# Sigmoid products, a Relu kept in PSUM and a key mask added by TensorE, in a hybrid decoder layer

## The chip, the cores and the metric

The kernel runs on one NeuronCore of a Trainium2 chip. The metric is the device time of one execution in microseconds (us). Engines are named as in the profile: PE is TensorE (matrix products), PEld its weight loads, DVE is VectorE, ACT is ScalarE, POOL is GpSimd, and SP is the engine whose queue issues most DMAs.

## The reference

One layer for 512 tokens of width 1024: a half-step SwiGLU, a mixer with two attention groups of 8 heads of 64, a second half-step SwiGLU, each with norms and modulation around it. The change touches the mixer alone. What it must compute there:

```
# group A: an indexer chooses 128 keys for each query, softmax over those
sc    = relu(einsum('bthd,bsd->bths', q_idx, k_idx))
score = where(causal, einsum('bths,bth->bts', sc, w_idx), -inf)
idx   = top_k(score, 128)
logits = q.k[idx] * D**-0.5 + rel_bias[t5_bucket(t - idx)]   # -inf where t - idx < 0
out   = softmax(logits) @ v[idx]

# group B: stick-breaking attention
z     = q.k * D**-0.5            # keys s < t only
A[t,s] = sigmoid(z_ts) * prod over s < j < t of sigmoid(-z_tj)
out   = A @ v
```

## The kernel before

Everything is float32; a product keeps its precision by three TensorE passes over operands split into a rounded high part (type fp32r) and a remainder (L271 to L273). A row block is 128 queries, `i` = 0 to 3, and it sees `L = 128 * (i + 1)` keys, so a head has four blocks of 128, 256, 384 and 512 columns, 1280 in all.

The mixer runs in this order. First the indexer (`indexer`): for 8 index heads and blocks `i` = 1 to 3 it forms 24 score tiles. Each is two products into a PSUM bank (L787, L788), a Relu by ACT from the bank into an SBUF tile `rl` (L734), and a product with the head's weight added to the running score by DVE (L735). Then `topk` takes the 128 largest of each row in sixteen rounds of MAX8 and MATCH_REPLACE8 on DVE (L766, L769) and leaves `notsel`, a bf16 tile with 1 where a key is not chosen (L772).

Then come eight units of two heads: units 0 to 3 are group B, 4 to 7 group A. While a unit's attention runs, the projections q, k, v of the next unit are slipped in between by `fill` (groups of L271 to L273), so PE has work whenever the attention waits. The weights of these projections are split by ACT or POOL and POOL (L132, L133, L138 `wl<-raw,wh`). The topk rounds have no data to wait for in group B and are slipped in on DVE there.

A block of a group B head (`attn_b`): two products and a bf16 product that masks the diagonal block (L895), then `Abs`, `Exp`, `Ln` on ACT (L897 to L899), `max(z, 0)` on ACT or DVE (L901, L903), a sum from the right by a scan on DVE (L904, two SBUF inputs), a subtraction (L905) and a last `Exp` on ACT (L906).

A block of a group A head (`attn_a`): DVE first builds `b` = bias window + mask in SBUF for all four blocks (L919, two SBUF inputs). Then two products (L787, L788), an addition with a running maximum (L926, which the profile calls CUSTOM_DVE_ANT_0), a negation of the maximum (L928) and `Exp` with the sum of the row on ACT (L929).

After that, in both groups, PE turns the weights around (L882), ACT and DVE split them (L132, L138 `pt`), and PE multiplies by v (L857). At the change of groups `bias_windows` makes the bias windows `U` by way of DRAM and `o_norm` normalizes group B's output (POOL's power, L143, then L574, L202, L577).

The order on each engine is set when the program is built, by a scheduler that hoists what it thinks is ready; on the chip each engine runs its list in order. Tiles come from pools. Those that matter: three PSUM banks `at` hold score tiles, attention tiles and the product with v; three SBUF tiles `p` of 128x1280 are shared by `x` and `y` in group B and by `p` and `b` in group A; `rl` has three buffers.

Of the kernel before, what the change touches and what calls it, by code (L numbers as in the profile page):

```python
# [13 lines left out]
F32 = mybir.dt.float32  # L14
F32R = mybir.dt.float32r
BF16 = mybir.dt.bfloat16
AF = mybir.ActivationFunctionType
ALU = mybir.AluOpType
# [5 lines left out]
NT = S // 128  # L24
# [6 lines left out]
NEG = -1e30  # L31
# [6 lines left out]
P_OFF = [0, 128, 384, 768]  # L38
# [26 lines left out]
class Block:  # L65
# [605 lines left out]
    def indexer(self):  # L671

        nc, pool, pj, at, tp, small, n = self.nc, self.pool, self.pj, self.at, self.tp, self.small, self.n
        w_in, ident = self.d["w_in"], self.ident
        cm = pool.tile([128, 512], BF16, tag="cm", name="cm")
# [6 lines left out]
                            nc.gpsimd if j < 2 else None), 128) for j in range(3)]  # L682
        banks = [pj.tile([128, 512], F32, tag="mm", name="mm") for _ in range(3)]
        banks.append(at.tile([128, 512], F32, tag="at", name="at"))
        load = nc.scalar.preload_act_table_set("natural_log_exp_and_others")
        self.tc.keep_in_program_order(load)
        wix = pool.tile([128, NT, NH], F32, tag="wix", name="wix")
        ki, qi = [], []
# [38 lines left out]
        def scores(hd):  # L727
            def one(i):
                L = 128 * (i + 1)
                s = sco[i - 1][:, 0:L]  # L730
                ps = at.tile([128, 512], F32, tag="at", name="at")[:, 0:L]
                self.qk(ps, i, hd % 2, qi[hd // 2], (kih, kih), (kil, kil), True)
                rl = pool.tile([128, 512], F32, tag="w2", name="rl", bufs=3)[:, 0:L]
                nc.scalar.activation(rl, ps, AF.Relu)  # L734
                nc.vector.scalar_tensor_tensor(s, rl, wix[:, i, hd:hd + 1], cm[:, 384 - 128 * i:512] if hd == 0 else s,  # L735
                                               op0=ALU.mult, op1=ALU.add)
            return [lambda i=i: one(i) for i in range(1, NT)]

        w3 = self.w_cols(w_in, C_QI + 384, 128)
        ps = pj.tile([128, 512], F32, tag="mm", name="mm")  # L740
# [9 lines left out]
        notsel, tops = [self.tri_gt], []  # L750
        for i in range(1, NT):
            L = 128 * (i + 1)
            ns = pool.tile([128, 512], BF16, tag=f"ns{i}", name="ns")
            tops.append(self.topk(sco[i - 1][:, 0:L], ns[:, 0:L]))
            notsel.append(ns)
# [130 lines left out]
    def attn_b(self, hd, qk):  # L886

        nc, pool, at = self.nc, self.pool, self.at
        x = pool.tile([128, 1280], F32, tag="p", name="x", bufs=3)
        y = pool.tile([128, 1280], F32, tag="p", name="y", bufs=3)  # L890
        for i in range(NT):
            L = 128 * (i + 1)
            ps = at.tile([128, 512], F32, tag="at", name="at")
            self.qk(ps[:, 0:max(256, L)], i, hd, *qk, False)
            nc.tensor.matmul(ps[:, 128 * i:L], self.negi, self.tri_ge, start=False, stop=True)  # L895
            z, xs, ys = ps[:, 0:L], x[:, P_OFF[i]:P_OFF[i] + L], y[:, P_OFF[i]:P_OFF[i] + L]
            nc.scalar.activation(xs, z, AF.Abs)  # L897
            nc.scalar.activation(xs, xs, AF.Exp, scale=-1.0)
            nc.scalar.activation(xs, xs, AF.Ln, bias=1.0)  # L899
            if i < 2:  # L900
                nc.scalar.activation(ys, z, AF.Relu)  # L901
            else:
                nc.vector.tensor_scalar(ys, z, 0.0, None, op0=ALU.max)  # L903
            nc.vector.tensor_tensor_scan(ys[:, ::-1], ys[:, ::-1], xs[:, ::-1], 0.0, op0=ALU.add, op1=ALU.add)  # L904
            nc.vector.tensor_sub(xs, z, ys)  # L905
            nc.scalar.activation(xs, xs, AF.Exp)  # L906
            self.fill()
        return x

    def attn_a(self, hd, qk, bias, notsel, den):  # L910

        nc, pool, at, small = self.nc, self.pool, self.at, self.small
        p = pool.tile([128, 1280], F32, tag="p", name="p", bufs=3)
        mx = small.tile([128, 4], F32, tag="mx", name="mx", bufs=2)
        nm = small.tile([128, 4], F32, tag="nm", name="nm", bufs=2)
        b = pool.tile([128, 1280], F32, tag="p", name="b", bufs=3)
        for i in range(NT):
            L = 128 * (i + 1)
            nc.vector.scalar_tensor_tensor(b[:, P_OFF[i]:P_OFF[i] + L], notsel[i][:, 0:L], NEG,  # L919
                                           bias[:, 0:L][:, ::-1], op0=ALU.mult, op1=ALU.add)  # L920
        for i in range(NT):
            L = 128 * (i + 1)
            ps = at.tile([128, 512], F32, tag="at", name="at")
            self.qk(ps[:, 0:max(256, L)], i, hd, *qk, True)
            pp = p[:, P_OFF[i]:P_OFF[i] + L]
            nc.vector.tensor_tensor_reduce(out=pp, in0=ps[:, 0:L], in1=b[:, P_OFF[i]:P_OFF[i] + L], scale=1.0,  # L926
                                           scalar=-3e38, op0=ALU.add, op1=ALU.max, accum_out=mx[:, i:i + 1])
            nc.vector.tensor_scalar(nm[:, i:i + 1], mx[:, i:i + 1], -1.0, None, op0=ALU.mult)  # L928
            nc.scalar.activation(pp, pp, AF.Exp, bias=nm[:, i:i + 1], accum_out=den[:, i, hd:hd + 1])  # L929
            self.fill((0, 1, 1, 2)[i])  # L930
        return p

# [33 lines left out]
```

## Time and profile before

| | us |
|---|---|
| median of 3 runs | 1123.7 (1123.42 to 1124.68) |
| the profiled execution, its own time | 1124.37 |
| its span | 1122.6 |
| PE busy | 1064.0 (95%) |
| DVE busy | 627.5 (56%) |
| ACT busy | 433.4 (39%) |
| POOL busy | 168.8 (15%) |

The first SwiGLU and the mixer's norm end near 430 us, the indexer runs to about 483, group B to about 604, group A to about 712, and the output projection and the second SwiGLU fill the rest. A matrix product of 512 columns is shown as about 395 ns long, but the next one starts 230 ns later, so the durations overlap: the start times tell what PE delivers, and a busy PE may still be held up.

### The profile page before, as it was taken

What the parts mean: (1) busy time and instruction counts of PE and PEld (TensorE: products, weight loads), DVE (VectorE), ACT (ScalarE), POOL (GpSimd) and SP (SyncE); (2) the same over time, 40 slices, a digit from 0 to 9 for tenths busy, and PEclk for the clock granted to TensorE, in tenths of its full rate; (3) what the DMA queues carried; (4) which work ended last, traced back from release to release, by engine and by line L of the source; (5) the groups of instructions that cost most, each with busy time, mean ns of one, the idle gap of its engine ahead of it and who ended that gap; (6) DMA issues with size and microseconds to landing.
All of it is one profiled execution on the core that took longest, in us unless ns stands there. A gap on an engine that the chain in (4) does not pass through costs nothing.

```text
span 1122.6 us, 13433 instructions
## 1 busy us (share of the span) xinstructions
PE 1064.0 (95%) x5079; PEld 871.7 (78%) x5079; DVE 627.5 (56%) x1055; ACT 433.4 (39%) x790; POOL 168.8 (15%) x116
## 2 busy tenths in 40 slices
PE   3889999999999999999998989989999999999997
PEld 2767888888888878867776778779888888888886
DVE  5969898744223165599999756574333333332313
ACT  3323222232212354477774656454223322221220
POOL 2120000000000433423333421422000000000030
PEclk9889999999999999999999999999999999999999
DMA  9967897833222503523334333413233333322222
GB/s 281 283 200 242 292 303 256 273 102 94 93 94 94 161 20 77 149 71 99 99 102 128 99 99 111 139 38 112 69 102 94 94 94 95 104 100 95 95 76 76
DMA packets 171365, 146.07 MB, mean 130 GB/s; under 512 B 7132, under 2 KB 142460, under 8 KB 171300
## 3 DMA queue, kind: packets, MB, share of 16 engines
q1 hardware_dynamic: 169792, 142.97, 41.8%
q10 hardware_dynamic: 1508, 2.24, 0.7%
q8 instruction: 40, 0.66, 0.2%
q14 instruction: 25, 0.20, 0.1%
HBM read 132.04 MB, written 2.13 MB: 120 GB/s over the span
## 4 chain that ended last, share of the span: by engine, by line
PE 75%; DVE 15%; issue 3%; ACT 2%; SPq 2%; POOL 1%; DMA 1%; DVEq 0%; POOLq 0%; ACTq 0%
PE mm L273 14%; PE mm L271 14%; PE mm L272 14%; PE mm L314 7%; PE mm L315 7%; PE mm L313 7%; PE mm L293 3%; PE mm L466 3%; DVE tk L769 2%; DVE y L904 2%; DVE m L766 2%; DVE pt L138 1%; DVE h L339 1%; DVE b L919 1%; SPq L420 1%
## 5 line engine op out<-in xcount | busy, mean ns | idle before, releaser
L132 ACT ACTIVATE wh<-raw 128x1024 fp32r<-128x1024 f32 x156 | 164.3, 1057 | 450.3 <-PE mm L272 153.0
L271 PE MATMUL mm<-nl,wh 128*128 128x512 f32 x808 | 320.3, 396 | 0.0
L272 PE MATMUL mm<-nh,wh 128*128 128x512 f32 x808 | 317.4, 393 | 0.0
L273 PE MATMUL mm<-nh,wl 128*128 128x512 f32 x808 | 317.3, 393 | 0.0
L138 DVE TENSOR_TENSOR wl<-raw,wh 128x1024 fp32r<-128x1024 f32 (+1 forms) x116 | 142.3, 1227 | 222.3 <-ACT wh L132 222.2
L273 PEld LDWEIGHTS mm<-nh,wl 128*128 128x128 f32 x808 | 152.3, 188 | 30.9
L271 PEld LDWEIGHTS mm<-nl,wh 128*128 128x128 f32 x808 | 152.7, 189 | 29.1
L272 PEld LDWEIGHTS mm<-nh,wh 128*128 128x128 f32 x808 | 152.5, 189 | 28.6
L314 PE MATMUL mm<-wh,hT 128*128 128x512 f32 x352 | 138.6, 394 | 0.0
L315 PE MATMUL mm<-wh,hT 128*128 128x512 f32 x352 | 138.6, 394 | 0.0
L138 POOL TENSOR_TENSOR wh<-raw,wh 128x1024 fp32r<-128x1024 f32 x10 | 25.5, 2561 | 594.7 <-ACT wh L132 594.7
L313 PE MATMUL mm<-wl,hT 128*128 128x512 f32 x288 | 113.7, 395 | 0.0
L138 POOL TENSOR_TENSOR wl<-raw,wh 128x1024 fp32r<-128x1024 f32 x31 | 75.0, 2423 | 166.9 <-ACT wh L132 156.6
L514 DVE TENSOR_TENSOR sg<-sg,mm 128x512 f32<-128x512 f32 x44 | 30.1, 685 | 106.7 <-PE mm L273 90.9
L315 PEld LDWEIGHTS mm<-wh,hT 128*128 128x128 f32 x352 | 66.3, 188 | 15.2
L314 PEld LDWEIGHTS mm<-wh,hT 128*128 128x128 f32 x352 | 66.3, 188 | 15.1
L153 DVE SCALAR_TENSOR_TENSOR acc<-ra,sc,acc 128x1024 f32<-128x1024 f32 x49 | 62.7, 1280 | 5.9 <-DMA ra<-in_w_ada_dram 5.2
L313 PEld LDWEIGHTS mm<-wl,hT 128*128 128x128 f32 x288 | 54.3, 188 | 12.7
L466 PE MATMUL mm<-nh,wh 128*128 128x512 f32 x96 | 36.0, 454 | 7.3 <-ACT nh L445 7.0
L787 PE MATMUL at<-kq 128*128 128x256 f32 (+2 forms) x88 | 31.3, 360 | 5.5 <-DVE mx L926 2.0
L138 DVE TENSOR_TENSOR hT<-sg,hT 128x512 fp32r<-128x512 f32 x44 | 31.9, 725 | 1.8 <-ACT hT L132 1.8
L132 ACT ACTIVATE hT<-sg 128x512 fp32r<-128x512 f32 x44 | 27.8, 632 | 13.3 <-DVE sg L514 13.3
(213 smaller groups left out, 1343.3 us busy)
## 6 DMA issues: line engine op xcount, KB each, us to landing
ra<-in_w_ada_dram SPq DMA_DIRECT2D x56, 512.0 KB, 5.2
raw<-in_w_ffn_gate_dram SPq DMA_DIRECT2D x44, 512.0 KB, 3.7
raw<-in_w_ffn_up_dram SPq DMA_DIRECT2D x44, 512.0 KB, 3.7
raw<-in_w_ffn_down_dram SPq DMA_DIRECT2D x44, 512.0 KB, 3.4
raw<-in_w_in_dram SPq DMA_DIRECT2D x28, 512.0 KB, 3.7
kq<-kq SPq DMA_DIRECT2D x84, 128.0 KB, 3.3
ra<-in_w_ada_dram SPq DMA_DIRECT2D x32, 256.0 KB, 5.5
raw<-in_w_out_dram SPq DMA_DIRECT2D x8, 512.0 KB, 3.8
```

The source lines that it names most:

```text
L132: return self.nc.scalar.activation(hi, src, AF.Copy)
L138: return a, (eng or self.nc.vector).tensor_sub(lo, src, hi.bitcast(F32))
L153: nc.vector.scalar_tensor_tensor(acc, raw, sc[:, k:k + 1], acc, op0=ALU.mult, op1=ALU.add)
L271: nc.tensor.matmul(ps[0:m, c], w[0][:, k, :], n[1][:, k, c], start=k == 0, stop=False)
L272: nc.tensor.matmul(ps[0:m, c], w[0][:, k, :], n[0][:, k, c], start=False, stop=False)
L273: return nc.tensor.matmul(ps[0:m, c], w[1][:, k, :], n[0][:, k, c], start=False, stop=k == KD - 1)
L293: mm = self.nc.tensor.matmul(ps[0:m, c], wt[:, k, :], nt[:, k, c], start=j + k == 0, stop=j == 2 and k == KD - 1)
L313: nc.tensor.matmul(ps, lh[:, t], wl, start=n == 0, stop=False)
L314: nc.tensor.matmul(ps, ll[:, t], wh, start=False, stop=False)
L315: nc.tensor.matmul(ps, lh[:, t], wh, start=False, stop=n == len(ks) - 1)
L466: nc.tensor.matmul(banks[j], ws[j][l][:, k, :], n[r][:, k, :], start=k + o == 0, stop=k == KD - 1 and o == 2)
L787: nc.tensor.matmul(ps, q[hd][:, t], kl[hd][:, 0:n], start=True, stop=False)
```

## The change

Four edits. The Relu of a score tile is written back into its PSUM bank, and DVE's weighted sum reads it there. Group B's weights are formed as products: sigmoid(z) to SBUF, sigmoid(-z) in place in the bank, a running product from the right (a scan with the multiplier 1, in place in the bank; its second input is a column of ones), and a product of the two, shifted by one column. Group A's mask is added by a third product, bf16 `negi` (the unit matrix times -1e30) with `notsel`, straight into the bank; DVE then adds the bias window, negates and takes the minimum in one instruction, and the exponential takes scale -1. The tables preloaded on ACT before the mixer are those with Sigmoid instead of those with Exp and Ln.

```diff
--- before.py
+++ after.py
@@ -682,7 +682,7 @@
                             nc.gpsimd if j < 2 else None), 128) for j in range(3)]
         banks = [pj.tile([128, 512], F32, tag="mm", name="mm") for _ in range(3)]
         banks.append(at.tile([128, 512], F32, tag="at", name="at"))
-        load = nc.scalar.preload_act_table_set("natural_log_exp_and_others")
+        load = nc.scalar.preload_act_table_set("sigmoid_and_others")
         self.tc.keep_in_program_order(load)
         wix = pool.tile([128, NT, NH], F32, tag="wix", name="wix")
         ki, qi = [], []
@@ -730,9 +730,8 @@
                 s = sco[i - 1][:, 0:L]
                 ps = at.tile([128, 512], F32, tag="at", name="at")[:, 0:L]
                 self.qk(ps, i, hd % 2, qi[hd // 2], (kih, kih), (kil, kil), True)
-                rl = pool.tile([128, 512], F32, tag="w2", name="rl", bufs=3)[:, 0:L]
-                nc.scalar.activation(rl, ps, AF.Relu)
-                nc.vector.scalar_tensor_tensor(s, rl, wix[:, i, hd:hd + 1], cm[:, 384 - 128 * i:512] if hd == 0 else s,
+                nc.scalar.activation(ps, ps, AF.Relu)
+                nc.vector.scalar_tensor_tensor(s, ps, wix[:, i, hd:hd + 1], cm[:, 384 - 128 * i:512] if hd == 0 else s,
                                                op0=ALU.mult, op1=ALU.add)
             return [lambda i=i: one(i) for i in range(1, NT)]
 
@@ -887,23 +886,17 @@
 
         nc, pool, at = self.nc, self.pool, self.at
         x = pool.tile([128, 1280], F32, tag="p", name="x", bufs=3)
-        y = pool.tile([128, 1280], F32, tag="p", name="y", bufs=3)
         for i in range(NT):
             L = 128 * (i + 1)
             ps = at.tile([128, 512], F32, tag="at", name="at")
             self.qk(ps[:, 0:max(256, L)], i, hd, *qk, False)
             nc.tensor.matmul(ps[:, 128 * i:L], self.negi, self.tri_ge, start=False, stop=True)
-            z, xs, ys = ps[:, 0:L], x[:, P_OFF[i]:P_OFF[i] + L], y[:, P_OFF[i]:P_OFF[i] + L]
-            nc.scalar.activation(xs, z, AF.Abs)
-            nc.scalar.activation(xs, xs, AF.Exp, scale=-1.0)
-            nc.scalar.activation(xs, xs, AF.Ln, bias=1.0)
-            if i < 2:
-                nc.scalar.activation(ys, z, AF.Relu)
-            else:
-                nc.vector.tensor_scalar(ys, z, 0.0, None, op0=ALU.max)
-            nc.vector.tensor_tensor_scan(ys[:, ::-1], ys[:, ::-1], xs[:, ::-1], 0.0, op0=ALU.add, op1=ALU.add)
-            nc.vector.tensor_sub(xs, z, ys)
-            nc.scalar.activation(xs, xs, AF.Exp)
+            z, xs = ps[:, 0:L], x[:, P_OFF[i]:P_OFF[i] + L]
+            nc.scalar.activation(xs, z, AF.Sigmoid)
+            nc.scalar.activation(z, z, AF.Sigmoid, scale=-1.0)
+            nc.vector.tensor_tensor_scan(z[:, ::-1], z[:, ::-1], self.ones.to_broadcast([128, L]), 1.0,
+                                         op0=ALU.mult, op1=ALU.mult)
+            nc.vector.tensor_mul(xs[:, 0:L - 1], z[:, 1:L], xs[:, 0:L - 1])
             self.fill()
         return x
 
@@ -911,22 +904,16 @@
 
         nc, pool, at, small = self.nc, self.pool, self.at, self.small
         p = pool.tile([128, 1280], F32, tag="p", name="p", bufs=3)
-        mx = small.tile([128, 4], F32, tag="mx", name="mx", bufs=2)
         nm = small.tile([128, 4], F32, tag="nm", name="nm", bufs=2)
-        b = pool.tile([128, 1280], F32, tag="p", name="b", bufs=3)
-        for i in range(NT):
-            L = 128 * (i + 1)
-            nc.vector.scalar_tensor_tensor(b[:, P_OFF[i]:P_OFF[i] + L], notsel[i][:, 0:L], NEG,
-                                           bias[:, 0:L][:, ::-1], op0=ALU.mult, op1=ALU.add)
         for i in range(NT):
             L = 128 * (i + 1)
             ps = at.tile([128, 512], F32, tag="at", name="at")
-            self.qk(ps[:, 0:max(256, L)], i, hd, *qk, True)
+            self.qk(ps[:, 0:max(256, L)], i, hd, *qk, False)
+            nc.tensor.matmul(ps[:, 0:L], self.negi, notsel[i][:, 0:L], start=False, stop=True)
             pp = p[:, P_OFF[i]:P_OFF[i] + L]
-            nc.vector.tensor_tensor_reduce(out=pp, in0=ps[:, 0:L], in1=b[:, P_OFF[i]:P_OFF[i] + L], scale=1.0,
-                                           scalar=-3e38, op0=ALU.add, op1=ALU.max, accum_out=mx[:, i:i + 1])
-            nc.vector.tensor_scalar(nm[:, i:i + 1], mx[:, i:i + 1], -1.0, None, op0=ALU.mult)
-            nc.scalar.activation(pp, pp, AF.Exp, bias=nm[:, i:i + 1], accum_out=den[:, i, hd:hd + 1])
+            nc.vector.tensor_tensor_reduce(out=pp, in0=ps[:, 0:L], in1=bias[:, 0:L][:, ::-1], scale=-1.0,
+                                           scalar=3e38, op0=ALU.add, op1=ALU.min, accum_out=nm[:, i:i + 1])
+            nc.scalar.activation(pp, pp, AF.Exp, scale=-1.0, bias=nm[:, i:i + 1], accum_out=den[:, i, hd:hd + 1])
             self.fill((0, 1, 1, 2)[i])
         return p
```

On DVE, where group A's first head begins, this stood before (`no`, `oT` belong to group B's norm; ISA is the addition with maximum, L926, and its read of the accumulator):

```order
L577 TENSOR_TENSOR no<-tp,col_100 128x512 x3
L919 SCALAR_TENSOR_TENSOR b<-tri_gt,U 128x128
L919 SCALAR_TENSOR_TENSOR b<-ns,U 128x256
L919 SCALAR_TENSOR_TENSOR b<-ns,U 128x384
L919 SCALAR_TENSOR_TENSOR b<-ns,U 128x512
L926 ISA p,mx<-at,b 128x128
L926 ISA mx 128x1
L926 ISA p,mx<-at,b 128x256
L926 ISA mx 128x1
L928 TENSOR_SCALAR nm<-mx 128x1
```

and this stands there now:

```order
L574 TENSOR_SCALAR ob<-ob,rstd 128x512
L577 TENSOR_TENSOR no<-tp,col_100 128x512
L914 ISA p,nm<-at,U 128x128
L914 ISA nm 128x1
L914 ISA p,nm<-at,U 128x256
L914 ISA nm 128x1
L914 ISA p,nm<-at,U 128x384
L914 ISA nm 128x1
L914 ISA p,nm<-at,U 128x512
L914 ISA nm 128x1
```

The four instructions that built `b` and the negations are gone, and the first addition follows the norm directly.

On PE, the last products of group B's heads are followed by the first of group A's. Before (`hot`, `rb` belong to the bias windows, `vt` and `ot` are turned tiles of v and of the output):

```order
L826 MATMUL tp<-ident,vt 128x128 x4
L865 MATMUL tp<-ident,ot 128x128 x4
L658 MATMUL mm<-hot,rb 8x128
L787 MATMUL at<-kq 128x256
L788 MATMUL at<-kq 128x256
L787 MATMUL at<-kq 128x256
L788 MATMUL at<-kq 128x256
L787 MATMUL at<-kq 128x384
L788 MATMUL at<-kq 128x384
L271 MATMUL mm<-nl,wh 128x512
```

and now:

```order
L786 MATMUL at<-kq 128x256
L787 MATMUL at<-kq 128x256
L912 LDWEIGHTS negi
L912 MATMUL at<-tri_gt,negi 128x128
L786 MATMUL at<-kq 128x256
L787 MATMUL at<-kq 128x256
L912 LDWEIGHTS negi
L912 MATMUL at<-ns,negi 128x256
L786 MATMUL at<-kq 128x384
L787 MATMUL at<-kq 128x384
L912 LDWEIGHTS negi
L912 MATMUL at<-ns,negi 128x384
```

Each pair is followed by the mask product, and from the second on that product reads `ns`, the tile that topk leaves.

On ACT, the same place. Before:

```order
L665 DMA U<-scr 128x512 x8
L132 ACTIVATE oT<-no 128x4x128 x3
L929 ACTIVATE p,den<-p,nm 128x128
L929 ACTIVATE p,den<-p,nm 128x256
L929 ACTIVATE p,den<-p,nm 128x384
L132 ACTIVATE oT<-no 128x4x128
```

and now:

```order
L665 DMA U<-scr 128x512 x8
L132 ACTIVATE oT<-no 128x4x128 x3
L916 ACT_TABLE_LOAD
L916 ACTIVATE p,den<-p,nm 128x128
L132 ACTIVATE oT<-no 128x4x128
L916 ACTIVATE p,den<-p,nm 128x256
```

Sigmoid and Exp lie in different tables, so a table load stands before group A's first exponential that was not there.

## Rows read from the trace of the kernel before

**Rows 1.** Chain of waits, the page's part 4: shares of the span by engine
```profile
PE 75%; DVE 15%; issue 3%; ACT 2%; SPq 2%; POOL 1%; DMA 1%; DVEq 0%; POOLq 0%; ACTq 0%
```

**Rows 2.** Busy time by stretch; us, busy us by engine, clock, DMA share, GB/s
```profile
470.00:486.00 16.00, 14.30 (x64) 11.27 (x64) 13.40 (x18) 9.66 (x26) 7.13 (x4) 0.89 0.36 99
486.00:604.00 118.00, 113.29 (x588) 85.77 (x587) 116.41 (x265) 88.01 (x209) 38.06 (x20) 1.00 0.36 95
604.00:712.00 108.00, 100.41 (x527) 81.77 (x526) 70.81 (x194) 60.58 (x141) 34.31 (x18) 0.98 0.42 119
```

**Rows 3.** Waits of PE, 470 to 486 us: total, times, longest
```profile
PE at L787 <- ACT rl L734: 1.7, 1, 1.7
```

**Rows 4.** Waits of PE, 486 to 604 us
```profile
PE tp L882 <- DVE pt L138: 2.6, 5, 0.9
PE tp L882 <- ACT x L906: 1.5, 6, 0.4
PE at L787 <- DVE x L905: 0.4, 1, 0.4
```

**Rows 5.** Waits of PE, 604 to 712 us
```profile
PE at L787 <- DVE mx L926: 2.0, 1, 2.0
PE tp L882 <- ACT p L929: 1.8, 2, 1.4
PE at L787 <- DMA kq<-kq: 1.4, 1, 1.4
PE tp L202 <- DVE ob L574: 1.4, 1, 1.4
PE tp L882 <- DVE pt L138: 1.0, 2, 0.8
```

**Rows 6.** Instructions of L735: duration ns min/median/max, first and last start
```profile
L735 DVE SCALAR_TENSOR_TENSOR sco<-rl,wix,sco x21: 472/620/2825, 455.5 to 482.7; 128x256 f32<-128x256 f32 x7, 128x384 f32<-128x384 f32 x7, 128x512 f32<-128x512 f32 x7
```

**Rows 7.** Timeline of POOL, 450 to 482 us: start us, us, instruction, idle before
```profile
476.71 2.39 POOL L138 TENSOR_TENSOR wl<-raw,wh 128x1024 fp32r<-128x1024 f32 x1
```

**Rows 8.** Timeline of DVE, 474 to 484 us
```profile
476.82 3.22 DVE L735 SCALAR_TENSOR_TENSOR sco<-rl,wix,sco 128x512 f32<-128x512 f32 x2 [1.31 <-ACT rl L734]
```

**Rows 9.** Timeline of PE, 477 to 486 us
```profile
480.39 0.50 PE L787 MATMUL at<-kq 128*128 128x512 f32 x1 [1.70 <-ACT rl L734]
...
483.07 0.63 PE L272 MATMUL mm<-nh,wh 128*128 128x512 f32 x1
```

**Rows 10.** Groups by line: busy us, mean ns of one, idle before
```profile
L904 DVE TENSOR_TENSOR_SCAN y<-y,x 128x128 f32<-128x128 f32 (+3 forms) x32 | 28.6, 895 | 0.5 <-ACT x L899 0.3
...
L919 DVE SCALAR_TENSOR_TENSOR b<-ns,U 128x256 f32<-128x256 bf16 (+2 forms) x24 | 18.3, 798 | 0.0
...
L903 DVE TENSOR_SCALAR y<-at 128x384 f32<-128x384 f32 (+1 forms) x16 | 9.6, 603 | 0.5 <-ACT x L897 0.5
```

**Rows 11.** Instructions of L926: duration ns min/median/max
```profile
L926 DVE CUSTOM_DVE_ANT_0 p<-at,b x32: 274/482/692, 612.9 to 697.4; 128x128 f32<-128x128 f32 x8, 128x256 f32<-128x256 f32 x8, 128x384 f32<-128x384 f32 x8, 128x512 f32<-128x512 f32 x8
```

**Rows 12.** Timeline of DVE, 594 to 616 us
```profile
597.99 2.67 DVE L772 TENSOR_TENSOR ns<-tk,sco 128x256 bf16<-128x256 f32 x2
...
609.35 3.67 DVE L919 SCALAR_TENSOR_TENSOR b<-ns,U 128x256 f32<-128x256 bf16 x3
```

**Rows 13.** Timeline of PE, 594 to 616 us
```profile
599.45 0.34 PE L788 MATMUL at<-kq 128*128 128x384 f32 x1
```

**Rows 14.** Timeline of ACT, 594 to 616 us
```profile
613.73 0.41 ACT L929 ACTIVATE p<-p,nm 128x128 f32<-128x128 f32 x1 [3.56 <-DVE nm L928]
```

**Rows 15.** Timeline of PE, 513 to 516 us
```profile
515.00 0.23 PE L895 MATMUL at<-tri_ge,negi 128*128 128x128 bf16 x1
...
515.36 0.40 PE L272 MATMUL mm<-nh,wh 128*128 128x512 f32 x1
515.59 0.39 PE L273 MATMUL mm<-nh,wl 128*128 128x512 f32 x1
```

**Rows 16.** Instructions of L685: duration ns min/median/max
```profile
L685 ACT ACT_TABLE_LOAD  x1: 1283/1283/1283, 417.7 to 417.7; - x1
```

## The prediction

> **What bounds the kernel now.** I read the chain of waits first. Three quarters of it is PE and 15% is DVE [rows 1], so an edit on DVE or ACT is worth only what PE waits for them. Next come the stretches of the mixer [rows 2]: in the indexer's tail (470 to 486 us) PE's granted clock is 0.89; in group B (486 to 604) DVE is busy for 116.4 of 118 us while PE, too, is shown busy for 113.3; in group A (604 to 712) DVE is at 70.8 of 108 and PE at 100.4. The last view is PE's waits in each stretch, since they are the most that this change can give back: 1.7 us in the tail [rows 3], 2.6 + 1.5 + 0.4 = 4.5 in group B [rows 4], 2.0 + 1.8 + 1.4 + 1.4 + 1.0 = 7.6 in group A [rows 5].
>
> Some of these waits come from one thing: a DVE instruction that lasts far longer than its shape asks. L735 takes 0.47 us at the least and 2.83 at the most [rows 6]; the two that begin at 476.82 need 3.22 us together [rows 8], while POOL runs a subtraction from 476.71 to 479.10 [rows 7]. PE then resumes at 480.39 after waiting 1.70 for ACT, whose `rl` tiles DVE had not freed, and a product at 483.07 is 0.63 long instead of 0.40 [rows 9, 15]: the clock had fallen to its lower level (1.2 of 2.4 GHz) after PE's idle time. The same shows at the head of group A, where three L919 take 3.67 us from 609.35 [rows 12] and PE's longest wait, 2.0 for L926, follows [rows 5].
>
> L926 adds one input from PSUM to one from SBUF, and none of its 32 is over 0.69 us [rows 11]. L735, L904 and L919 have both inputs in SBUF. After the change the first two have one in PSUM and the third is gone. The Trainium skill (SBUF — State Buffer, "Who interferes with whom") says that a DVE instruction with at most one SBUF input, outside the 2-port modes, does not contend with GpSimd. The rows of L926 and L735 agree; for a scan no row here shows it.
>
> **The indexer.** The Relu keeps its duration and stays in the bank. What goes is the hold on L735, and with it the wait of 1.7 and the slow clock behind it, 0.11 x 16 = 1.8 us of lost full speed. What comes is that a bank is busy until DVE has read it, not only until ACT has: three banks in place of three banks and three `rl` tiles. PE's next pair, and the projections behind it in its list, wait for that. Between nothing and the whole 3.5 I take 3.0.
>
> **Group B.** Per block ACT gives up Abs, Exp, Ln and the last Exp (and two of four Relus) for two Sigmoids. ACT is at 88 of 118 us, so this is worth nothing by itself, but the turning products that waited 1.5 for L906 now wait for a DVE product directly. On DVE the sixteen L903 go: 9.6 us [rows 10]. The subtraction becomes a product of the same shape (PSUM and SBUF in, SBUF out, one column fewer): no difference. The scan now reads and writes PSUM, which no row shows. From below, one pass at L926's mean, 0.48; from above, today's 0.895 and such a pass on top, 1.38 [rows 10, 11]. I take 0.90, the row of the same operation. DVE then has 9.6 us less in a stretch that it fills, and PE can get back at most its 4.5 of waits. Since DVE still has about 107 us to do there, I take 3.5.
>
> `x` alone now takes one of the three `p` tiles per head, so the next head can begin earlier; that is part of the same 3.5.
>
> **Group A.** The L919 go, 18.3 us for 24 of the 32 [rows 10], and the negations. DVE was not full there, so what counts is the waits behind them: 2.0, 1.8 and 1.0 = 4.8 [rows 5], and the clock, 0.02 x 108 = 2.2 us. Two waits stay: 1.4 for the norm's L574, whose chain through POOL is untouched, and 1.4 for a DMA of q and k. Gain 7.0.
>
> The price is on PE: 32 mask products. In group B such a product of 128 columns is there today: it starts at 515.00, the second product after it at 515.36 and the third 0.23 later [rows 15], so it costs 0.36 - 0.23 = 0.13 us. At 0.23 us per 512 columns the other lengths come to 0.19, 0.25 and 0.30; a head to 0.87, eight to 7.0. If the extra 0.07 that belongs to the weights and not to the columns is hidden behind the longer products, it is 1280 x 0.23 / 512 = 0.575 a head, 4.6 in all. I take 5.8, all of it on PE's path.
>
> The mask also brings a wait: PE now needs `ns`, so topk's end, right after the first products of group A; behind it stand the k projection of the next unit and the norm's transposes. Today PE is through these products at 599.79 [rows 13] and the two `ns` end at 600.66 [rows 12], so PE would lose about 0.9. With 9.6 us off DVE and 3.5 off PE before that point, DVE arrives some 5 us ahead, and I count nothing. If the scan is slower than taken, this is where it shows.
>
> A table load appears before the first exponential of group A. The one in the trace takes 1.28 us [rows 16]. ACT idles 3.56 before that exponential today [rows 14], so a load fits in and is hidden, though the earlier start that I count on is cut into. The Trainium skill (ScalarE: Activation LUTs, "What ACT_TABLE_LOAD costs") puts a switch at 2.66 us, with 1.38 of drain after the load; the row shows only the load. By the page the sum would be up to 1.4 us worse, by the row nothing.
>
> **The sum.** A product that follows a wait is itself 0.10 longer (0.50 at 480.39 against 0.40, rows 9 and 15); with some 15 waits gone that is 1.5 us. So 3.0 + 3.5 + 7.0 + 1.5 - 5.8 = 9.2 us. The profiled execution took 1124.37 (span 1122.6, 1.8 around it, which stays): 1115.2. It lies 0.7 above the median of 1123.7, so the median to expect is 1114.5, rounded to **1115**. The rivals' times are medians too.
>
> **Rivals.**
> *All the cover holds.* Every wait of rows 3 to 5 but the DMA's goes (12.4), so does the slow clock (4.0), and the mask costs 4.6 with 1.5 of restarts saved: 13.3 less, 1110.4. For it: the waits are few and each has a DVE instruction behind it. Against it: DVE remains nearly full in group B. Chance 0.17.
>
> *DVE stays last in group B.* With a scan at 1.38, DVE there has 116.4 - 9.6 + 32 x 0.48 = 122.2 us, 5.8 more than now; PE stops at the first `ns` for what DVE is late. Then 3.0 + 7.0 + 0.7 - 5.8 - 5.8 = -0.9: 1124.6, no change. With three quarters of that surcharge it is 1.9 more than now and 1120.7; with half of it or less the stretch shrinks and the forecast holds. For it: DVE is the full engine there. Against it: L926 pays nothing visible for reading PSUM. Chance 0.17.
>
> *The table load is exposed.* If ACT comes to the load only when the first addition is done, its whole 1.28 lies on the path, once, and as much is missing from the 7.0: 9.2 - 1.3 = 7.9, so 1115.8. Against it: ACT's 3.56 of idle time in that place [rows 14]. Chance 0.10. With the drain that the page of the Trainium skill adds it would be 1117.2.
>
> *The banks run out in the indexer.* Each of 24 score tiles holds its bank for DVE's median 0.62 longer [rows 6]. If PE pays it every time, that is 14.9 us against the 9.2 won: 1129.4, slower. It decides if tiles come faster than a third of a bank's cycle: two products at 0.23, a Relu of about DVE's 0.62 (an estimate) and that 0.62, 1.7 us, so one tile in 0.57. The 21 of rows 6 start 27.2 us apart from first to last, 1.36 each; only the last few come faster. Chance 0.07.
>
> **How the numbers follow.** The forecast, some 1112 to 1118, has 0.49, the first rival 0.17, the second 0.17, the table load 0.10, the banks 0.07. The range runs from 1109 (a little under the first rival) to 1122 (beyond the second at three quarters of its surcharge); outside it I leave 0.2, most of it above. From no change a measurement here can tell about 0.2%, 2.2 us. The forecast, the first rival and the table load are faster, and half of the second: 0.84. The other half of the second is no change: 0.09. The banks are slower: 0.07.
>
> **What would show it.** Right: no L734 or score sum over 0.8 us beside a POOL subtraction; the clock of the indexer's tail and of group A's head near 1.00; DVE visibly below full in group B and topk done before PE asks for `ns`; PE's start-to-start cost of a mask product at 0.13 to 0.30 us; the end of group A about 9 us earlier, and everything after it unchanged in length. Wrong: scans over 1 us on average, a PE wait for `ns`, PE waits for `at` banks in the indexer, or the first exponential of group A waiting for its table.

## The result, and the profile after

The changed kernel takes 1114.85 us in the median of five runs (1112.37 to 1117.54) against 1123.7: ratio 0.9923, 95% interval 0.9905 to 0.9941. The forecast was 1115. The execution profiled here is the slowest of the five (1117.54, span 1115.7); a second set of runs (e11 below) gave 1113.61.

First the chain of waits, the page's part 4: shares of the span by engine.

```profile
PE 81%; DVE 8%; issue 3%; DMA 3%; ACT 2%; POOL 1%; SPq 0%; DVEq 0%; POOLq 0%; ACTq 0%
```

Against [rows 1] DVE has lost almost half of its share, PE has 6 points more, and DMA has gone from 1% to 3%. The stretches of the mixer, in the columns of [rows 2]:

```profile
470.00:486.00 16.00, 16.00 (x81) 13.41 (x80) 8.90 (x17) 9.38 (x21) 7.10 (x4) 1.00 0.52 145
486.00:596.00 110.00, 105.00 (x562) 82.39 (x560) 106.61 (x249) 58.99 (x128) 37.01 (x20) 1.00 0.36 97
596.00:704.00 108.00, 106.54 (x575) 86.41 (x579) 50.69 (x129) 63.40 (x146) 34.60 (x19) 1.00 0.42 121
```

The clock is 1.00 throughout; it was 0.89 in the tail and 0.98 in group A. In group B DVE is still nearly full, 106.6 of 110 us. PE's waits in group B, 486 to 596 us (total, times, longest):

```profile
PE tp L881 <- DVE x L899: 2.3, 5, 0.6
PE at L786 <- DMA kq<-kq: 2.2, 3, 0.8
PE tp L881 <- ACT x L895: 0.3, 1, 0.3
```

And in group A, 596 to 704 us:

```profile
PE at L786 <- DMA kq<-kq: 1.3, 1, 1.3
PE tp L881 <- DVE pt L138: 0.2, 1, 0.2
```

In the tail (470 to 486) PE waits for nothing. In group A 7.6 us [rows 5] became 1.5. In group B the sum has not fallen, 4.8 against 4.5 [rows 4]: PE waits less for DVE and ACT and comes early to the q and k tiles, whose DMA is not yet done. Now the instructions that the change touches (duration ns min/median/max, first and last start us), the score sum, the scan, and group A's addition:

```profile
L734 DVE SCALAR_TENSOR_TENSOR sco<-at,wix,sco x21: 473/616/752, 458.8 to 485.1; 128x256 f32<-128x256 f32 x7, 128x384 f32<-128x384 f32 x7, 128x512 f32<-128x512 f32 x7
...
L897 DVE TENSOR_TENSOR_SCAN at<-at,ones x32: 403/810/1232, 485.8 to 581.8; 128x128 f32<-128x128 f32 x8, 128x256 f32<-128x256 f32 x8, 128x384 f32<-128x384 f32 x8, 128x512 f32<-128x512 f32 x8
...
L914 DVE CUSTOM_DVE_ANT_0 p<-at,U x32: 279/488/692, 604.5 to 690.8; 128x128 f32<-128x128 f32 x8, 128x256 f32<-128x256 f32 x8, 128x384 f32<-128x384 f32 x8, 128x512 f32<-128x512 f32 x8
```

For the score sum and the addition the minima and medians are within 6 ns of those of before [rows 6, 11]. What went is the maximum of the score sum: 0.75 us in place of 2.83. Two timelines at the change of groups (start us, us, instruction): first ACT,

```profile
604.58 0.63 ACT L132 ACTIVATE oT<-no 128x512 fp32r<-128x512 f32 x1 [0.36 <-DVE no L577]
605.23 1.28 ACT L916 ACT_TABLE_LOAD   x1
606.52 0.40 ACT L916 ACTIVATE p<-p,nm 128x128 f32<-128x128 f32 x1
```

then PE.

```profile
596.28 0.23 PE L912 MATMUL at<-tri_gt,negi 128*128 128x128 bf16 x1
...
596.65 0.28 PE L912 MATMUL at<-ns,negi 128*128 128x256 bf16 x1
```

PE reaches the first mask of topk at 596.65 and has not waited. The table load follows the instruction ahead of it without idle time and delays the first exponential by its 1.28 us, yet no wait of PE for ACT's `p` is left in group A.

To compare kernels, the mixer is cut by the start times of PE's instructions: *a* runs from the first score product to group B's first turning product, *b* to group A's first score product, *c* to the last product with v, *d* to the end of the span. All in us:

| kernel | first score product | a | b | c | d | median |
|---|---|---|---|---|---|---|
| before | 448.87 | 39.45 | 110.37 | 108.34 | 415.54 | 1123.7 |
| after, this profile | 452.16 | 35.67 | 108.10 | 104.33 | 415.43 | 1114.85 |
| e11: after again | 449.62 | 35.68 | 108.03 | 104.34 | 415.44 | 1113.61 |
| e1: Relu | 449.47 | 36.07 | 110.89 | 111.07 | 415.28 | 1124.57 |
| e2: sigmoid | 447.16 | 39.39 | 108.27 | 108.57 | 415.23 | 1120.32 |
| e3: mask | 448.17 | 39.43 | 110.33 | 106.63 | 415.41 | 1122.66 |
| e4: Relu, sigmoid | 449.08 | 35.79 | 107.59 | 108.52 | 415.27 | 1118.04 |
| e5: Relu, mask | 448.84 | 35.97 | 110.95 | 106.95 | 415.42 | 1118.97 |
| e6: sigmoid, mask | 449.91 | 39.31 | 108.46 | 104.35 | 415.51 | 1117.64 |
| e7: before, no subtraction | 444.80 | 35.99 | 107.59 | 101.59 | 417.26 | 1107.83 |
| e12: after, no subtraction | 445.75 | 35.68 | 107.33 | 102.59 | 415.37 | 1108.66 |
| e9: after, scan in SBUF | 450.43 | 35.85 | 121.59 | 104.27 | 415.71 | 1127.77 |
| e10: after, no mask | 448.43 | 35.67 | 108.17 | 99.32 | 415.64 | 1109.63 |
| e8: after, mask on DVE | 446.83 | 35.68 | 108.13 | 99.54 | 417.89 | 1110.29 |

From before to e11: a -3.8, b -2.3, c -4.0, d -0.1, in all 10.2 behind the first score product. The time of the first score product varies from 446.8 to 452.2 among the kernels that do the same work ahead of it; the 3.3 that the profiled execution lost there are not the change's (e11 lost 0.75). The stretches *a* to *d* leave this out, so they tell more than the medians do, but each comes from one execution.

### The profile page after: what moved, and what is told of

Its sections match the earlier page's. It is cut to its first block, busy times and chain, and to the rows that moved or that the text cites. A ratio compares the mean times of both kernels' runs of the same rounds, so it can differ in the third digit from the quotient of the medians.

```text
span 1115.7 us, 13371 instructions
## 1 busy us (share of the span) xinstructions
PE 1063.1 (95%) x5107; PEld 872.9 (78%) x5111; DVE 590.8 (53%) x975; ACT 406.0 (36%) x711; POOL 167.5 (15%) x116
## 4 chain that ended last, share of the span: by engine, by line
PE 81%; DVE 8%; issue 3%; DMA 3%; ACT 2%; POOL 1%; SPq 0%; DVEq 0%; POOLq 0%; ACTq 0%
PE mm L271 15%; PE mm L273 15%; PE mm L272 15%; PE mm L314 8%; PE mm L315 8%; PE mm L313 7%; PE mm L293 3%; PE mm L466 3%; DMA ra<-in_w_ada_dram 2%; DMA kq<-kq 1%; DVE at L897 1%; PE at L786 1%; PE tp L881 1%; PE at L787 1%; DVE h L339 1%
## 5 line engine op out<-in xcount | busy, mean ns | idle before, releaser
L313 PEld LDWEIGHTS mm<-wl,hT 128*128 128x128 f32 x288 | 54.1, 188 | 13.1
L138 DVE TENSOR_TENSOR pt<-tp,pt 128x512 fp32r<-128x512 f32 (+1 forms) x48 | 27.2, 594 | 18.9 <-ACT pt L132 18.8
```

The lines of the kernel that those rows point to most:

```text
L138: return a, (eng or self.nc.vector).tensor_sub(lo, src, hi.bitcast(F32))
L313: nc.tensor.matmul(ps, lh[:, t], wl, start=n == 0, stop=False)
```

## The experiments

The kernel before ran beside each set; its medians there were 1123.62 (e1 to e4), 1123.77 (e5 to e8) and 1122.79 (e9 to e12). Ratios are to those runs.

### One edit alone, and two (e1 to e6)

**e1**, the Relu edit alone.

```
-                rl = pool.tile([128, 512], F32, tag="w2", name="rl", bufs=3)[:, 0:L]
-                nc.scalar.activation(rl, ps, AF.Relu)
-                nc.vector.scalar_tensor_tensor(s, rl, wix[:, i, hd:hd + 1], cm[:, 384 - 128 * i:512] if hd == 0 else s,
+                nc.scalar.activation(ps, ps, AF.Relu)
+                nc.vector.scalar_tensor_tensor(s, ps, wix[:, i, hd:hd + 1], cm[:, 384 - 128 * i:512] if hd == 0 else s,
```

> The kernel before with the Relu edit alone. Theory H (what the change gives back are holds: DVE instructions with two SBUF inputs kept waiting by POOL's subtractions): no score sum longer than 0.8 us, PE's wait of 1.7 in the indexer's tail and its low clock gone, 1 to 3 us less in all (1121 to 1123); group B and group A as in the kernel before. Theory W (what counts is the amount of DVE work removed): the Relu edit removes none, so no measurable difference (within 0.2%).

Measured: 1124.57, ratio 1.0009 (1.0000 to 1.0018): no gain. By the total theory W is right. The trace says something else: the score sums are at most 0.75 us, the tail's wait and low clock are gone, and *a* is 3.4 shorter. It is given back, 0.5 in *b* and 2.7 in *c*. The place is group A's second unit, at the additions of mask and bias for its second head. In the kernel before these were not held:

```profile
637.52 0.27 DVE L919 SCALAR_TENSOR_TENSOR b<-tri_gt,U 128x128 f32<-128x128 bf16 x1
637.78 1.48 DVE L919 SCALAR_TENSOR_TENSOR b<-ns,U 128x256 f32<-128x256 bf16 x3
```

POOL's timeline there, in e1:

```profile
623.92 4.75 POOL L138 TENSOR_TENSOR wl<-raw,wh 128x1024 fp32r<-128x1024 f32 x2 [0.54 <-ACT wh L132]
628.63 1.09 POOL L133 TENSOR_SCALAR wh<-raw 128x1024 fp32r<-128x1024 f32 x1
629.80 2.44 POOL L138 TENSOR_TENSOR wl<-raw,wh 128x1024 fp32r<-128x1024 f32 x1
```

DVE's, with the old additions of mask and bias (L918 in this kernel):

```profile
627.02 1.79 DVE L918 SCALAR_TENSOR_TENSOR b<-tri_gt,U 128x128 f32<-128x128 bf16 x1
628.74 0.14 DVE L927 TENSOR_SCALAR nm<-mx 128x1 f32<-128x1 f32 x1
628.80 4.46 DVE L918 SCALAR_TENSOR_TENSOR b<-ns,U 128x256 f32<-128x256 bf16 x3
```

PE's:

```profile
633.92 0.44 PE L881 MATMUL tp<-ident,p 128*128 128x128 f32 x2 [1.30 <-DVE v L138]
636.13 0.69 PE L881 MATMUL tp<-ident,p 128*128 128x128 f32 x2 [1.77 <-ACT p L928]
```

And the stretch around it, in the columns of [rows 2]:

```profile
630.00:642.00 12.00, 8.72 (x33) 6.62 (x32) 8.45 (x19) 3.45 (x8) 2.24 (x1) 0.74 0.30 85
```

The rows show a chain: the additions now fall on POOL's subtractions and take 6.25 us together instead of 1.75, the turning products wait 1.30 and 1.77 for what is queued behind them, and the granted clock of the stretch drops to 0.74, a mean of its two levels (1.2 and 2.4 GHz). So a gain of 3.4 us met a stall downstream that depends on when the additions start. That is not only a matter of arriving earlier: PE reached group A 2.3 us before the old time, but these additions start 10.5 us before it, because DVE's list, too, came out in another order. No run separates the two.

**e2**, the sigmoid edit alone (the core of it; the table loaded ahead changes with it).

```
-            nc.scalar.activation(xs, z, AF.Abs)
...
-            nc.vector.tensor_sub(xs, z, ys)
-            nc.scalar.activation(xs, xs, AF.Exp)
+            nc.scalar.activation(xs, z, AF.Sigmoid)
+            nc.scalar.activation(z, z, AF.Sigmoid, scale=-1.0)
...
+            nc.vector.tensor_mul(xs[:, 0:L - 1], z[:, 1:L], xs[:, 0:L - 1])
```

> The kernel before with the sigmoid edit of group B alone (and the table that is loaded ahead for it). The changed kernel's trace shows group B, from its first scan to the first addition of group A, 10.9 us shorter. Theory H: two parts of that are holds, of score sums that run into group B and of the first three additions of group A, so B alone is worth 5 to 8 us: 1116 to 1119. Theory W: all of it is the work removed in group B (9.6 us of Relu on DVE), so 9 to 11 us less: 1113 to 1115, and A unchanged in length.

Measured: 1120.32, ratio 0.9970 (0.9959 to 0.9982), less than either theory said. *b* is 2.1 shorter and *c* not at all (108.57): the old additions are still there, and in 594 to 704 us PE waits 4.0 for ACT's `p`, up to 1.8 at a time. The additions that are held in e1 are held here as well:

```profile
625.23 4.47 DVE L913 SCALAR_TENSOR_TENSOR b<-ns,U 128x256 f32<-128x256 bf16 x3
```

**e3**, group A's edit alone.

```
-            nc.vector.scalar_tensor_tensor(b[:, P_OFF[i]:P_OFF[i] + L], notsel[i][:, 0:L], NEG,
-                                           bias[:, 0:L][:, ::-1], op0=ALU.mult, op1=ALU.add)
...
+            nc.tensor.matmul(ps[:, 0:L], self.negi, notsel[i][:, 0:L], start=False, stop=True)
```

> The kernel before with the edit of group A alone: 32 mask products on PE in place of 32 additions of bias and mask on DVE (18.3 us of DVE work beside holds). The prediction's terms were +7.0 for the waits and the clock and -5.8 for PE, with the wait for the last topk uncovered here (0.9): between 0.3 and 1.2 us less, no measurable difference (1122.5 to 1124). Theory W: DVE was at 70.8 of 108 there, its work is worth nothing, and the products cost 5 to 7 us: 1128 to 1131, slower. A third result, 1115 to 1119, would say that the waits behind the additions were worth twice what their rows show.

Measured: 1122.66, ratio 0.9990 (0.9981 to 0.9998), as the prediction's terms said. PE's waits from 597 to 640 us show the wait for topk that was counted as covered in the full change:

```profile
PE at L919 <- DVE ns L772: 0.7, 1, 0.7
PE tp L202 <- DVE ob L574: 0.5, 1, 0.5
```

It is 0.7 against the 0.9 worked out ahead, and both rows are absent from the changed kernel.

**e4**, the Relu and sigmoid edits (e1's and e2's lines), group A as before.

> The changed kernel with group A as before: Relu and sigmoid edits, no mask products. The prediction's terms give 7.0 less for the waits that return and 5.8 more for PE that is free of the products: 1115 to 1117, within 0.2% of the changed kernel. Theory W: the products are the one price of the change, so without them 1108 to 1110. The changed kernel's own trace (group A, from first to last addition, 1.7 us longer than before) speaks for something between: 1113.

Measured: 1118.04, ratio 0.9945 (0.9932 to 0.9957): 3.2 above the changed kernel, a little over the first expectation and 5 over the 1113 that the trace seemed to say; theory W is out. *c* is 108.5 against 104.3. Against e2 the Relu edit gives 4.3 us behind the first score product, although group A keeps its additions. So an earlier arrival is not always lost on them: e2 had already paid for the hold shown there, and it is paid once.

**e5**, the Relu edit and group A's (e1's and e3's lines), group B as before.

> Relu edit and group A's edit, group B as before. Theory H: the Relu edit alone gained 3 us up to the start of group A (PE's first product of A 2.9 us earlier after the first score product) and lost them in A's second unit, where three additions of bias and mask were held by POOL for 1.5, 0.8 and 2.2 us. With the mask on PE there is nothing to hold, so the 3 us stay: 1119 to 1120.5, that is 3 to 4 less than before, where the two edits alone gave -0.95 and +0.96 (sum: no gain). Theory W: additive, 1123.6, no measurable difference.

Measured: 1118.97, ratio 0.9964 (0.9951 to 0.9976). Two edits that alone give +0.95 and -0.96 give -4.8 together. *a* keeps its 3.5 and *c* is 106.95 in place of e1's 111.07. Theory H had put it at 1119 to 1120.5, theory W at 1123.6.

**e6**, the sigmoid edit and group A's, the old Relu (e1's lines the other way round).

> The changed kernel with the old Relu, whose result goes to SBUF: score sums with two SBUF inputs. Theory H: the hold of the last score sums returns, PE waits 1.7 in the indexer's tail and comes to group B's first turn 3.4 to 3.8 us later; nothing downstream absorbs it: 1118 to 1119. Theory W and additivity (Relu alone is worth nothing, +0.95): 1114 to 1115, as the changed kernel.

Measured: 1117.64, ratio 0.9948 (0.9934 to 0.9961), a little under theory H's 1118 and well over W's 1115. The score sums (duration ns min/median/max) are those of before,

```profile
L735 DVE SCALAR_TENSOR_TENSOR sco<-rl,wix,sco x21: 469/619/2842, 456.5 to 483.7; 128x256 f32<-128x256 f32 x7, 128x384 f32<-128x384 f32 x7, 128x512 f32<-128x512 f32 x7
```

and so is PE's wait from 470 to 486 us:

```profile
PE at L787 <- ACT rl L734: 1.7, 1, 1.7
```

*a* is 39.3, and *b* and *c* are within 0.4 of the changed kernel's. With the other two edits in place the Relu edit is worth 4.1 us behind the first score product (e11 against e6), beside the sigmoid edit alone 4.3 (e4 against e2); by itself it was worth 0.4 there (e1).

### The holds by themselves (e7, e12, e9)

**e7** and **e12**: POOL's subtraction left out, in the kernel before and in the changed one.

```
+        if lo == "none":
+            self.rounded(wh, raw, hi)
+            return view(wh), view(wh)
         self.split(wh, wl, raw, lo, hi)
```

> The kernel before, without POOL's subtractions for the low parts of the indexer's and the projections' weights (18 of 2.4 us between 486 and 712 us, and two in the indexer): the high part stands in for the low part, so the projections are not the reference's. DVE, ACT and PE do all that they did. Theory H: the holds of score sums, scans and additions go, and with them the waits and low clock behind them: 5 to 8 us less, 1115.5 to 1118.5, with L735 and L919 at no more than 0.8 us. Theory W: DVE has the same work, so no measurable difference, 1122.5 to 1124.5.

> The changed kernel without POOL's subtractions for the low parts of the indexer's and the projections' weights (the high part stands in, so the projections are not the reference's): the same edit took 15.9 us off the kernel before, 4 of them ahead of the first score product and 11.3 behind it. Theory H: the change has already ended most of the holds behind that point, so the edit is worth 4 ahead of it and 0 to 3 behind it: 1107.5 to 1111. Rival (the change works by less DVE work, and the subtractions cost something else): the two gains add up, 1098 to 1101.

Measured: e7 1107.83, ratio 0.9862 (0.9848 to 0.9875), 15.9 us less where theory H had 5 to 8; e12 1108.66, ratio 0.9879 (0.9864 to 0.9893), inside H's range. In e7 the score sums, scans and additions, with unchanged shapes and inputs, last (ns min/median/max):

```profile
L738 DVE SCALAR_TENSOR_TENSOR sco<-rl,wix,sco x21: 474/619/753, 451.5 to 476.5; 128x256 f32<-128x256 f32 x7, 128x384 f32<-128x384 f32 x7, 128x512 f32<-128x512 f32 x7
...
L907 DVE TENSOR_TENSOR_SCAN y<-y,x x32: 409/814/1217, 477.2 to 577.4; 128x128 f32<-128x128 f32 x8, 128x256 f32<-128x256 f32 x8, 128x384 f32<-128x384 f32 x8, 128x512 f32<-128x512 f32 x8
...
L922 DVE SCALAR_TENSOR_TENSOR b<-ns,U x24: 407/552/1497, 598.4 to 672.0; 128x256 f32<-128x256 bf16 x8, 128x384 f32<-128x384 bf16 x8, 128x512 f32<-128x512 bf16 x8
```

So DVE's work was the same, and without the subtractions *a* fell by 3.5, *b* by 2.8 and *c* by 6.8 us (*d* grew by 1.7); what is left in L922's maximum belongs to other subtractions of POOL that stayed. In the changed kernel the same edit takes 0.0, 0.7 and 1.8 off. About 4 more us go ahead of the first score product in both; 1.9 of them are PE's wait for `k`, which falls from 2.8 to 0.9, and the rest is within what that time varies by. That is the clearest reading: most of what leaving out POOL's subtractions would have given, the change has already taken. In e12 PE no longer waits for the DMA of q and k (2.2 + 1.3 us in the changed kernel), but in *b* its waits for DVE's `x` rise from 2.3 to 4.4.

Read the other way, the two runs also say what the change is worth where these subtractions are missing: 0.3 in *a*, 0.3 in *b*, and a loss of 1.0 in *c* (e7 to e12). If the mask products cost there the 5.0 that e10 measures below, group A's edit still gives 4.0 in *c*. So not all of group A's gain is holds by these subtractions. In e7 PE still waits 2.0 once, at the first additions, which run beside another subtraction of POOL; how much of the 4.0 is such holds and how much DVE's work no run separates.

**e9**: the changed kernel with the scan and the product in SBUF.

```
+        yt = pool.tile([128, 1280], F32, tag="p", name="y", bufs=3)
-            nc.scalar.activation(z, z, AF.Sigmoid, scale=-1.0)
+            y = yt[:, P_OFF[i]:P_OFF[i] + L]
+            nc.scalar.activation(y, z, AF.Sigmoid, scale=-1.0)
...
-            nc.vector.tensor_mul(xs[:, 0:L - 1], z[:, 1:L], xs[:, 0:L - 1])
+            nc.vector.tensor_mul(xs[:, 0:L - 1], y[:, 1:L], xs[:, 0:L - 1])
```

> The changed kernel with group B's second sigmoid, scan and product in SBUF (two SBUF inputs each for scan and product; a second tile of the p ring per head, as before the change). Theory H: scans and products are held by POOL again, in about eight places (before: four scans, 2.6 us in all), and DVE is full there, so group B from PE's first product to group A's first is 1 to 4 us longer than the changed kernel's 111.9: 1116 to 1118. Rival (PSUM is the dearer place for the scan, and the bank is held longer by it): the scan is not over 0.80 us on average and the time is the same or up to 3 us less, 1112 to 1115.

Measured: 1127.77, ratio 1.0052 (1.0038 to 1.0066), slower than before. The direction is theory H's, the size three times its own. Groups of DVE (busy us, mean ns), in e9:

```profile
L899 DVE TENSOR_TENSOR_SCAN y<-y,ones 128x128 f32<-128x128 f32 (+3 forms) x32 | 31.4, 990 | 0.0
L901 DVE TENSOR_TENSOR x<-y,x 128x127 f32<-128x127 f32 (+3 forms) x32 | 16.7, 529 | 0.0
```

In the changed kernel:

```profile
L897 DVE TENSOR_TENSOR_SCAN at<-at,ones 128x128 f32<-128x128 f32 (+3 forms) x32 | 25.7, 817 | 0.2
L899 DVE TENSOR_TENSOR x<-at,x 128x127 f32<-128x127 f32 (+3 forms) x32 | 14.8, 476 | 0.0
```

Here is one such scan, by the timelines of POOL and DVE in e9, two scans that take 3.23 us together:

```profile
522.93 2.41 POOL L138 TENSOR_TENSOR wl<-raw,wh 128x1024 fp32r<-128x1024 f32 x1 [11.54 <-ACT wh L132]
...
523.51 3.23 DVE L899 TENSOR_TENSOR_SCAN y<-y,ones 128x256 f32<-128x256 f32 x2
```

The two groups carry 7.6 us more, and PE's waits for `x` grow to

```profile
PE tp L881 <- DVE x L901: 12.9, 14, 2.0
```

from 2.3 (482 to 608 us). That is 10.6 of the 13.5 by which *b* grew. The rival is out: the scan takes 0.99 us on average in SBUF against 0.82. Why 7.6 us of holds cost more than themselves is not settled: a head again takes two of the three `p` tiles, and DVE's list came out in another order, with topk's end ahead of the last scan (592.8 us) and not behind it. The experiment shows that a scan is held as the others are; it does not price one hold.

### The mask by itself (e10, e8, e11)

**e10**: the changed kernel without the mask products.

```
-            nc.tensor.matmul(ps[:, 0:L], self.negi, notsel[i][:, 0:L], start=False, stop=True)
```

> The changed kernel without group A's mask at all (its 32 products left out, so the scores are not masked): the price of the mask by itself. The prediction's 5.8 us (4.6 to 7.0) and the 6.3 from the start-to-start times say 1108.5 to 1110.5, and that the mask on DVE (1110.3) is then almost free. If PE's products are hidden by its waits, 1113 to 1115; if dropping the mask also shows that the mask on DVE costs waits, 1105 to 1108.

Measured: 1109.63, ratio 0.9887 (0.9871 to 0.9903), inside the first expectation. *c* is 5.0 shorter than in e11, 0.16 per product; the medians differ by 4.0.

**e8**: the mask added by DVE to the scores in PSUM.

```
-            nc.tensor.matmul(ps[:, 0:L], self.negi, notsel[i][:, 0:L], start=False, stop=True)
+            z = ps[:, 0:L]
+            nc.vector.scalar_tensor_tensor(z, notsel[i][:, 0:L], NEG, z, op0=ALU.mult, op1=ALU.add)
```

> The changed kernel with group A's mask on DVE instead of PE, but on the scores in PSUM (mask in bf16 from SBUF times -1e30 plus the scores, written back into the bank): one SBUF input, so by theory H no hold. PE loses 32 products, at 0.25, 0.12, 0.18 and 0.24 us a head (start to start in the changed kernel against the one with the old group A) = 0.79 x 8 = 6.3 us. DVE, at 49.4 of 104 us there, takes 32 more passes of 0.28 to 0.69, 15.4 us, and each lies in the chain from scores to exponential. If PE's list has enough other work in between: 1109 to 1111. If the longer chain shows as waits of the turning products for ACT's exponentials, 8 to 16 waits of 0.3 to 0.5, half or all of it is lost: 1112 to 1116.

Measured: 1110.29, ratio 0.9891 (0.9875 to 0.9906). This is faster than before, and its median is 3.3 below e11's, though the two intervals touch. The additions, one input from SBUF and one from PSUM, are not held (duration ns min/median/max):

```profile
L913 DVE SCALAR_TENSOR_TENSOR at<-ns,at x24: 410/556/693, 592.0 to 680.9; 128x256 f32<-128x256 bf16 x8, 128x384 f32<-128x384 bf16 x8, 128x512 f32<-128x512 bf16 x8
```

*c* is 99.54, 4.8 shorter than with the products and only 0.2 longer than with no mask: there the longer chain costs PE almost nothing. Half of the gain goes again in *d* (417.9 against 415.4), where the last head's output makes PE wait once (690 to 700 us):

```profile
PE tp L864 <- ACT ot L861: 1.8, 1, 1.8
```

**e11**: the changed kernel once more.

> The changed kernel once more, beside the others of this call. Its profiled execution lost 3.3 us in the unchanged first part. If that is variation from execution to execution, the median is 1114 to 1116 and this profile has the first score product at 446 to 450 us, as in the other kernels; if the change delays it, 452 again.

Measured: 1113.61, ratio 0.9919 (0.9903 to 0.9934), first score product at 449.62: variation, not the change. The median is 0.4 under the range expected.

## Why the prediction was right, and where it was not

| term (us) | predicted | shown | by |
|---|---|---|---|
| indexer | -3.0 | -3.8 | *a* |
| group B | -3.5 | -2.3 | *b* |
| group A, with the 1.5 of restarts | -8.5 | -9.0 | *c*, -4.0 less the mask's +5.0 |
| mask on PE | +5.8 | +5.0 | e10 against e11 |
| sum | -9.2 | -10.1 | |

**The indexer** was right in cause and size. The wait, the low clock behind it and the hold go together: e6 has all three, e1 and the changed kernel none. The banks do not run out: PE has no wait there.

**Group B** was right in sign, but not in the way. The prediction had PE get back most of its 4.5 us of waits; in sum they did not shrink (4.8), since PE came early to the q and k tiles and waited 2.2 us for their DMA, which the prediction had counted once, in group A. Yet *b* is 2.3 shorter. Here is that stretch before and in e11, in the columns of [rows 2]:

```profile
488.32:598.70 110.38, 105.67 (x552) 79.57 (x550) 109.83 (x255) 83.59 (x198) 36.85 (x20) 1.00 0.37 97
485.31:593.33 108.02, 103.17 (x552) 81.12 (x551) 104.64 (x245) 58.08 (x126) 36.91 (x20) 1.00 0.36 99
```

PE is busy 2.5 us less with as many products and the same clock, so what went are delays too short to show as idle time; which instructions had caused them is open. DVE did not become visibly less than full (97% of the stretch), a sign that the prediction had asked for. The scan came at 0.82 us against the 0.90 taken, and with that the second rival fell. The waits that stayed kept the first rival, in which all cover holds, from coming true.

**Group A** was right as a sum. The wait of 1.4 for the norm's L574 was said to stay and went; e3 and e5 keep part of it (0.5 and 1.0 us), and in group A of the kernels with the sigmoid edit it is absent. The wait for `ns` did not come, and e3 shows the 0.7 that it costs without that lead. The 1.5 of restarts, set at some 15 waits gone, was counted too high: the views before show 20 waits of PE and those after 11, so 9 went, 0.9 us at the prediction's own price, which no run tests. The table load did delay the first exponential. That is one of the prediction's signs of being wrong and the condition of its third rival, and the 3.56 us of idle time that were to hide the load were not there. It cost no visible wait of PE, which the prediction had not foreseen: that the time held is in part luck. The Trainium skill (ScalarE: Activation LUTs, "What ACT_TABLE_LOAD costs") adds a drain of 1.38 us to the load; in this trace the ACTIVATE before it ends 0.02 us ahead of the load and the next starts 0.01 us after it, so the row decided rightly.

**The step that failed** is one that the sum took for granted: that the terms are independent. Alone, the three edits give +0.95, -3.3 and -0.96 against the runs beside them, 3.3 in all; together they give 9. Behind the first score product they give 0.4, 2.2 and 1.9 alone, 4.5 in all, and 10.2 together; taken out of the changed kernel one at a time (e6, e5 and e4 against e11) they are worth 4.1, 5.8 and 3.7, 13.6 in all. So no edit has a price of its own. The Relu edit is worth nothing only while both other groups are as before; beside the sigmoid edit or group A's it keeps most or all of its gain (e4, e5). Group A's edit is worth 1.7 us of *c* in the kernel before (e3), and 4.1 to 4.2 with any other edit in place (e1 to e5, e2 to e6, e4 to the changed kernel), because e1, e2 and e4 all run into the hold in group A's second unit (in e4, too, these four additions take 5.8 us from the first to the last), and with the mask on PE they are gone. With all three made at once, none of the additions is left on which an earlier arrival had been lost. That the sum came so near is in part luck: its terms are off by 0.5 to 1.2 us each, and the errors partly cancel.

**The cause** stands by e7 and e12: with DVE's work left as it was, leaving out POOL's subtractions gives 13.1 us from the first score product to the end of group A (3.5 + 2.8 + 6.8), and the change leaves 2.5 of them. It is shown for the indexer by e6 as well, and for the scan by e9. Open are the short delays that went in group B and up to 4 us of group A's gain. The Trainium skill (SBUF — State Buffer, "Who interferes with whom") says that a DVE instruction with two SBUF inputs contends with a GpSimd instruction that reads SBUF. The rows of L918 in e1 and of the scan in e9 agree; for the scan this was open before.

## What to carry to other kernels

When an instruction on one engine lasts several times what its shape asks, look at what runs beside it on the other engines before counting its work as the cost; here it was enough to let one of two inputs come from PSUM. A stall that depends on when two instructions meet can swallow a gain made further up, so an edit that is worth nothing alone may be worth its whole price next to another, and edits have to be tried in pairs. And where PE is the bound, work moved onto it costs what it takes (5.0 us here), while an engine with room may do it for less: 0.2 in group A and 2.3 once behind its last head.

## What the runs showed of the hardware that was not expected

- An instruction of 64 columns with a single SBUF tensor as input, a product with a per-row scalar, was held too. In the changed kernel, which leaves them as they were, eight of them (L709, duration ns min/median/max) last

```profile
L709 DVE TENSOR_SCALAR k<-kk,rstd x8: 241/244/2341, 440.9 to 444.1; 128x64 f32<-128x64 f32 x8
```

while POOL runs

```profile
441.26 2.40 POOL L138 TENSOR_TENSOR wl<-raw,wh 128x1024 fp32r<-128x1024 f32 x1 [0.42 <-ACT wh L132]
```

and without POOL's subtractions, in e12 (there L712), they last

```profile
L712 DVE TENSOR_SCALAR k<-kk,rstd x8: 249/249/254, 438.0 to 439.1; 128x64 f32<-128x64 f32 x8
```

It stands on PE's path in the indexer's head: PE waits 2.8 us for `k` in the kernel before and in the changed one, and 0.9 in e7 and e12. No kernel here tried to remove that hold alone.

- A scan takes the same time in PSUM as in SBUF: 403 ns at the least for 128 columns in the changed kernel and 407 for the same operation in e9.
